# The order of the steps in the second block's layers: matrix-memory projections moved from the front to the last delta-rule chains

## The chip, the cores and the metric

One core of a Trainium2 chip runs the whole program. The metric is the device time of one execution in microseconds (us). The engines are TensorE (PE in the profile), VectorE (DVE), ScalarE (ACT), GpSimd (POOL) and SyncE (SP, which starts the DMAs). Each engine carries out its own instructions in a fixed order and waits, in that order, for what an instruction needs.

## The reference

The model has two parts. The first block (two layers of mixers and a mixture of 16 experts) is not touched by the change. The second block has two layers on a sequence of 256 tokens by 1024 features; each layer has two branches over the same input and then a feed-forward network, with layer norms. Branch A is a matrix memory (mLSTM, 4 heads, keys of 128, values of 256); branch B is a gated delta rule (8 heads of 128) on convolved projections. Cut to what matters:

```
def _mlstm_chunked(q, k, v, i_pre, f_pre):           # 4 heads, chunks of 64
    ... num = (q k^T * w) v + sc * (q C);  C = carry * C + k^T v ...
def _causal_conv(u, w):                              # 4 taps, per feature
    return lax.conv_general_dilated(u, ..., padding=[(k - 1, 0)], ...)
def _gated_delta_chunked(q, k, v, beta, g):          # 8 heads, chunks of 64
    q = _l2norm(q) * (dk ** -0.5)
    k = _l2norm(k)
    ...
    sol = lax.linalg.triangular_solve(eye + a_low, rhs, ...)   # per chunk of 64
    u, w = sol[..., :dv], sol[..., dv:]
    def step(s_st, chunk):                           # four chunks, one after another
        v_new = uc - w @ s_st
        o = qe @ s_st + attn @ v_new
        s_new = s_st * g_end + kd^T @ v_new
        return s_new, o
```

Everything is in float32.

## The kernel before

**Projections.** `gemm_t` (L72) makes one output tile of 256 features by 256 tokens with 48 matmuls: 8 pieces of the inner dimension, two halves, and three products each, because input and weight are each split into a high and a low part (`xh`, `xl`, and `whl`, which ACT and DVE make from the loaded weight at L62 and L63). The result is built in a PSUM tile `acc`; there are two such tiles in all, so that a third projection tile can begin only when the first has been read out by its evacuation.

**Steps.** A layer of `block2` first makes the gate rows (`small_rows`, a chain of short row operations), then goes through the steps of `ORDER2` (L1033), then `branches` (gates and products of both branches), `down`, `norm`, `ffn`, `norm`. The steps are:
- `G n` (`gdn_proj`): three projection tiles q, k, v of two delta-rule heads. `conv_piece` (L1146) evacuates each: two ACT and six DVE operations with the taps into the tile `cva`, a tanh on ACT, two DVE operations into `KQ`, `kr` or `vr`. `cva` has two buffers; for q and k POOL puts the squares in it (L1207), and step R reads them there.
- `Z n` (`gdn_gate`): one more projection tile, the output gate.
- `R n` (`gdn`): the delta-rule chain of that pair of heads. PE sums the squares (`pss`, L1232), then come products (`pk`, `py`, ...), then five levels of a triangular inverse (tile `pi`: L1310, a copy on ACT, L1315 and L1319, a subtraction on DVE), then `pu` (L1327) and `pw` (L1335), then four chunks of the recurrence (L1347, a subtraction on DVE, L1351, L1358, L1364, an update of the state on DVE), a norm on DVE and the transposes `pot` (L1380). Nearly every step waits for the one ahead of it on another engine.
- `P j` (`ml_proj`): the matrix memory's projections for two of its heads: tiles `qT` and `kT` (one buffer each, so the second pair's evacuations at L1396 and L1397 wait until the first pair's heads have been read), two tiles `va0` and `va1` of 512 features, and two gate tiles.
- `M j` (`mlstm`): the matrix memory of these two heads, one head after the other (`pb`, `pst`, `pkt`, `pd`, `pn`, squares into `junk` on ACT at L1471, a norm, `pha`).

`junk` is one tile that takes the squares of R (L1368) and of M (L1471), so that these writes follow in program order.

**What sets the order.** The program's text order gives priorities and the order of waits on shared buffers; a scheduler then writes one fixed list of instructions for each engine, in which the matmuls of a chain stand between those of projections. The object `after` holds back the first projection of the second layer until an operation of the norm ahead of it has been issued.

Of the kernel before, what the change touches and what calls it, by code (L numbers as in the profile page):

```python
# [1029 lines left out]
ALPHA = 4.0 ** 0.25  # L1030
D_FF = 2816
LN_EPS = 1e-5
ORDER2 = "P0 G0 G1 Z0 R0 Z1 R1 G2 Z2 G3 Z3 M0 R2 R3 P1 M1"  # L1033

QA, KA, VA, OA, QB, KB, VB, ZB, GA, GB = 0, 512, 1024, 2048, 3080, 4104, 5128, 6152, 7192, 8216

# [636 lines left out]
def split_x(E, x):  # L1673

    nc, m, C = E.nc, E.m, E.c2
    xh = E.st.tile([128, 8, 256], FR, name="xh", tag="st")
    xl = E.st.tile([128, 8, 256], FR, name="xl", tag="st")
    for k2 in range(4):
        pt = m.tile([128, 2, 256], FT, name="pln", tag="mm")
        for j in range(2):  # L1680
            for t in range(2):
                k = 2 * k2 + j
                nc.tensor.transpose(pt[:, j, 128 * t:128 * t + 128], x[:, t, 128 * k:128 * k + 128], C.id)
        ks = slice(2 * k2, 2 * k2 + 2)
        nc.scalar.activation(xh[:, ks], pt, AF.Copy)
        nc.vector.tensor_sub(xl[:, ks], pt, xh[:, ks])
    return xh, xl


def block2(E, x):  # L1690
    tc = E.tc
    xh, xl = split_x(E, x)
    nl = E.nlayers
    after = contextlib.nullcontext()
    for l in range(nl):
        with tc.tile_pool(name=f"t2_{l}", bufs=2) as E.t2, tc.tile_pool(name=f"sm{l}", bufs=2) as E.sm, \
                tc.tile_pool(name=f"rw{l}", bufs=1) as E.rows:
            E.P = E.rows
            G = G2(E, l, x, xh, xl)
            G.params()  # L1700
            G.junk = E.rows.tile([128, 256], FT, name="junk")
            G.R = small_rows(E, l, xh, xl)
            G.hbh = E.st.tile([128, 8, 256], FR, name="hbh", tag="st")
            G.hbl = E.st.tile([128, 8, 256], FR, name="hbl", tag="st")
            G.hah = E.st.tile([128, 8, 256], FR, name="hah", tag="st")
            G.hal = E.st.tile([128, 8, 256], FR, name="hal", tag="st")
            zs = {}
            for step in ORDER2.split():
                k, n = step[0], int(step[1])
                if k == "G":  # L1710
                    zs[n] = G.gdn_proj(n)
                elif k == "Z":
                    G.gdn_gate(n, zs[n])
                elif k == "R":
                    G.gdn(n, zs[n])
                elif k == "P":
                    with after:
                        zs["m", n] = G.ml_proj(n)
                    after = contextlib.nullcontext()
                else:  # L1720
                    G.mlstm(n, zs["m", n])
            G.branches()
        with tc.tile_pool(name=f"ffn{l}", bufs=1) as E.F, tc.tile_pool(name=f"lnp{l}", bufs=1) as E.lnp:
            ps = G.down(E.i["w_out_2"][l], G.yh, G.yl, KC)
            xh, xl = G.norm(0, ps)
            ps = G.ffn(xh, xl)
            r = G.norm(1, ps, l == nl - 1)
        if r:
            xh, xl = r
            after = G.after[0]  # L1730
# [70 lines left out]
def program(tc, ins, out):  # L1801
    nc = tc.nc
    E = Env()
    E.tc, E.nc, E.i, E.nlayers, E.nomoe = tc, nc, ins, 2, False
    with tc.tile_pool(name="c", bufs=1) as E.cp, tc.tile_pool(name="w", bufs=3) as E.wp, \
            tc.tile_pool(name="hl", bufs=3) as E.hl:
        xt = E.cp.tile([128, 2, D], FT, name="x")
        with tc.tile_pool(name="c1", bufs=1) as c1, tc.tile_pool(name="st1", bufs=4) as E.st, tc.tile_pool(name="md", bufs=1) as E.md, \
                tc.tile_pool(name="sm1", bufs=1) as E.sm:
            ct = c1.tile([128, 2, D], FT, name="xc")  # L1810

            def load_ctx():
                nc.sync.dma_start(ct, ins["ctx"].rearrange("(t p) d -> p t d", p=128))
                load_consts1(E, c1)

            E.load_x = lambda: nc.sync.dma_start(xt, ins["x"].rearrange("(t p) d -> p t d", p=128))
            E.load_ctx = load_ctx
            block1(E, [xt, ct])
        with tc.tile_pool(name="c2", bufs=1) as c2, tc.tile_pool(name="st2", bufs=6) as E.st, tc.tile_pool(name="pacc2", bufs=2, space=PSUM) as E.acc, \
                tc.tile_pool(name="pm2", bufs=2, space=PSUM) as E.m:  # L1820
            load_consts2(E, c2)
            E.out = out
            block2(E, xt)
# [16 lines left out]
```

## Time and profile before

| | |
|---|---|
| device time, median of 3 runs | 2824.7 us (2815.96 to 2825.24) |
| profiled execution: its own time | 2826.67 us |
| profiled execution: span | 2824.9 us |
| granted TensorE clock, mean over the span | 0.96 of full |
| busy: PE / DVE / ACT / POOL | 89% / 48% / 29% / 9% of the span |
| steps and branches, layer 0 | 1525.40 to 1944.80 us |
| steps and branches, layer 1 | 2169.70 to 2599.40 us |

The span is what the trace covers; the profiled execution took 1.8 us more, and 2 us more than the median of the runs. The two stretches at the end of the table are the ones in which the change moves anything. In the trace a row of the timeline gives start, length, engine, line and tile, and in square brackets how long the engine stood idle ahead of it and for whom. Ends of matmuls are modelled, so distances from start to start are used for PE.

### The profile page before, as it was taken

Reading aid. Unit: us, or ns where it says so; the run is one execution under the profiler, and the core shown is the slowest. Engines: PE = TensorE matmul, PEld = TensorE weight load, DVE = VectorE, ACT = ScalarE, POOL = GpSimd, SP = SyncE. Lnnn points to the kernel's source line nnn. Section 1 sums busy time; section 2 is a strip of 40 time slices with the busy share of each in tenths; the row PEclk is TensorE's granted clock in tenths of the full one; section 3 lists DMA queues with packets and bytes.
Section 4 is the critical chain, followed back from the end, with each engine's and each line's share of the span. In section 5 each row is a group of like instructions: output and inputs, shape, how many; then the busy total and the mean of one; then the engine's idle time right before and its main releaser. Section 6 shows DMA issues by size and latency. Waiting matters only on the chain.

```text
span 2824.9 us, 42465 instructions
## 1 busy us (share of the span) xinstructions
PE 2527.0 (89%) x17771; PEld 1740.5 (62%) x17771; DVE 1354.1 (48%) x2663; ACT 818.2 (29%) x1339; POOL 243.5 (9%) x293
## 2 busy tenths in 40 slices
PE   6999989988889997666667999999999999999998
PEld 4776743322227662111114988888997888879996
DVE  4446533232236562001103768456656667556765
ACT  2334311000014430000002434334444433334442
POOL 1000110000000010000000122000202031100200
PEclk9999999999999999888899998999999998999999
DMA  7434469999995568999996421335654431325553
GB/s 292 180 120 147 164 272 421 422 421 421 421 381 181 185 242 360 422 421 421 421 421 264 155 91 53 113 111 175 209 181 138 152 118 46 105 90 194 179 192 121
DMA packets 237459, 665.60 MB, mean 236 GB/s; under 512 B 11572, under 2 KB 165860, under 8 KB 182356
## 3 DMA queue, kind: packets, MB, share of 16 engines
q1 hardware_dynamic: 235428, 657.81, 61.2%
q0 software_dynamic: 1696, 4.59, 0.5%
q8 instruction: 139, 2.28, 0.3%
q14 instruction: 52, 0.43, 0.0%
q10 hardware_dynamic: 144, 0.49, 0.0%
HBM read 661.78 MB, written 1.05 MB: 235 GB/s over the span
## 4 chain that ended last, share of the span: by engine, by line
PE 59%; DMA 24%; issue 9%; DVE 5%; POOL 2%; ACT 1%; SPq 0%; DVEq 0%; ACTq 0%; POOLq 0%
DMA w<-in_exp_w_up 8%; DMA w<-in_exp_w_down 8%; PE acc L84 6%; PE acc L86 6%; DMA w<-in_exp_w_gate 6%; PE acc L85 6%; PE pj L316 3%; PE pj L318 3%; PE pgate L862 3%; PE pj L317 3%; PE pd L862 2%; PE pup L862 2%; PE pada L182 2%; PE psc L435 1%; PE psc L451 1%
## 5 line engine op out<-in xcount | busy, mean ns | idle before, releaser
L63 DVE TENSOR_TENSOR whl<-w,whl 128x1024 fp32r<-128x1024 f32 x376 | 469.2, 1251 | 310.0 <-ACT whl L62 309.4
L62 ACT ACTIVATE whl<-w 128x1024 fp32r<-128x1024 f32 x376 | 396.2, 1058 | 472.3 <-PE acc L86 237.0
L84 PE MATMUL acc<-xh,whl 128*128 128x256 f32 x1664 | 476.5, 286 | 0.5 <-DVE xh L1619 0.5
L86 PE MATMUL acc<-xh,whl 128*128 128x256 f32 x1664 | 471.7, 283 | 0.2
L85 PE MATMUL acc<-xl,whl 128*128 128x256 f32 x1664 | 471.1, 283 | 0.0
L84 PEld LDWEIGHTS acc<-xh,whl 128*128 128x128 f32 x1664 | 316.7, 190 | 11.0 <-issue 6.5
L86 PEld LDWEIGHTS acc<-xh,whl 128*128 128x128 f32 x1664 | 316.4, 190 | 5.6 <-issue 3.6
L85 PEld LDWEIGHTS acc<-xl,whl 128*128 128x128 f32 x1664 | 316.8, 190 | 3.3 <-issue 2.5
L862 PE MATMUL pup<-w,xg 128*64 128x512 f32 (+1 forms) x1024 | 221.4, 662 | 67.9 <-DMA w<-in_exp_w_up 67.9
L862 PE MATMUL pgate<-w,xg 128*64 128x512 f32 (+1 forms) x1016 | 218.5, 648 | 45.8 <-DMA w<-in_exp_w_gate 43.4
L862 PE MATMUL pd<-w,ehT 128*64 128x512 f32 (+1 forms) x1024 | 202.7, 622 | 59.3 <-DMA w<-in_exp_w_down 42.3
L862 PEld LDWEIGHTS pup<-w,xg 128*64 128x64 f32 (+1 forms) x1024 | 52.6, 130 | 228.7 <-DMA w<-in_exp_w_up 149.6
L862 PEld LDWEIGHTS pd<-w,ehT 128*64 128x64 f32 (+1 forms) x1024 | 51.7, 125 | 186.5 <-DMA w<-in_exp_w_down 87.2
L862 PEld LDWEIGHTS pgate<-w,xg 128*64 128x64 f32 (+1 forms) x1016 | 50.9, 127 | 177.7 <-DMA w<-in_exp_w_gate 91.8
L316 PE MATMUL pj<-whl,hT 128*128 128x256 f32 x496 | 144.5, 292 | 6.1 <-ACT hT L300 5.8
L318 PE MATMUL pj<-whl,hT 128*128 128x256 f32 x496 | 143.3, 290 | 0.9 <-DVE hT L301 0.9
L317 PE MATMUL pj<-whl,hT 128*128 128x256 f32 x496 | 142.8, 289 | 0.0
L893 DVE TENSOR_TENSOR od<-pd,g 128x512 f32<-128x512 f32 x24 | 16.6, 691 | 232.0 <-PE pd L862 232.0
L881 DVE SCALAR_TENSOR_TENSOR et<-et,pup 128x512 f32<-128x512 f32 x24 | 16.5, 687 | 224.0 <-PE pup L862 223.8
L316 PEld LDWEIGHTS pj<-whl,hT 128*128 128x128 f32 x496 | 94.5, 191 | 24.7 <-issue 10.9
L317 PEld LDWEIGHTS pj<-whl,hT 128*128 128x128 f32 x496 | 94.5, 191 | 13.1 <-issue 8.9
L318 PEld LDWEIGHTS pj<-whl,hT 128*128 128x128 f32 x496 | 94.5, 191 | 8.5 <-issue 5.7
(607 smaller groups left out, 4158.9 us busy)
## 6 DMA issues: line engine op xcount, KB each, us to landing
w<-in_exp_w_down SPq DMA_DIRECT2D x128, 1024.0 KB, 19.8
w<-in_exp_w_up SPq DMA_DIRECT2D x127, 1024.0 KB, 19.8
w<-in_exp_w_gate SPq DMA_DIRECT2D x125, 1024.0 KB, 19.8
w<-in_w_in SPq DMA_DIRECT2D x82, 1024.0 KB, 5.1
w<-in_ada_w SPq DMA_DIRECT2D x48, 1024.0 KB, 6.4
w<-in_w_ffn_up SPq DMA_DIRECT2D x44, 1024.0 KB, 5.1
w<-in_w_ffn_down SPq DMA_DIRECT2D x22, 1024.0 KB, 4.8
w<-in_w_out SPq DMA_DIRECT2D x16, 1024.0 KB, 5.5
```

The lines of the kernel that those rows point to most:

```text
L62: nc.scalar.activation(h, w, AF.Copy)
L63: (engine or nc.vector).tensor_sub(lo, w, h)
L84: nc.tensor.matmul(ps[:, b], h[:, k], xh[:, k], start=(k == 0), stop=False)
L85: nc.tensor.matmul(ps[:, b], h[:, k], xl[:, k], start=False, stop=False)
L86: nc.tensor.matmul(ps[:, b], lo[:, k], xh[:, k], start=False, stop=(k == KC - 1))
L182: nc.tensor.matmul(self.ps[32 * j:32 * j + 32], self.st[:, k], ws[j], start=(k == 0), stop=(k == KC - 1), skip_group_check=True)
L316: nc.tensor.matmul(ps, xh, wh, start=start, stop=False, skip_group_check=bool(ks))
L317: nc.tensor.matmul(ps, xh, wl, start=False, stop=False, skip_group_check=bool(ks))
L318: nc.tensor.matmul(ps, xl, wh, start=False, stop=stop, skip_group_check=bool(ks))
L435: self.E.nc.tensor.matmul(o, wT[:, 128 * c:128 * c + 128], v[:, t0 + c, 64 * h:64 * h + 64], start=(c == 0), stop=(c == n // 128 - 1))
L451: nc.tensor.matmul(ps[:, :n], self.cqT[r, h // 2, 128 * t:128 * t + 128], self.ckT[r, h // 2, k0:k0 + n], start=True, stop=True)
L862: m = nc.tensor.matmul(ps[64 * h + mw * i:64 * h + mw * i + mw], lhs(kk, i, e), ws[i][k][:, 512 * h:512 * h + 512], start=(kk == 0), stop= ...
```

## The change

In both layers P0 moves from the front to a place between R2 and R3, M0 moves behind R3, and R2 comes ahead of it; the steps G0 to Z3 stay in their own order. The hold-back `after` moves with the first projection, which is now G0's. (The changed file has one more line, so its lines from 1034 to 1709 are one higher.)

```diff
-ORDER2 = "P0 G0 G1 Z0 R0 Z1 R1 G2 Z2 G3 Z3 M0 R2 R3 P1 M1"
+
+ORDER2 = "G0 G1 Z0 R0 Z1 R1 G2 Z2 G3 Z3 R2 P0 R3 M0 P1 M1"
...
                 if k == "G":
-                    zs[n] = G.gdn_proj(n)
+                    with after:
+                        zs[n] = G.gdn_proj(n)
+                    after = contextlib.nullcontext()
...
                 elif k == "P":
-                    with after:
-                        zs["m", n] = G.ml_proj(n)
-                    after = contextlib.nullcontext()
+                    zs["m", n] = G.ml_proj(n)
```

No instruction of a step is added or removed. What moves on the engines is shown at three places, all in layer 0.

**Place 1, PE, the last part of R3.** Before, the values' projection of P1 (`va0_12669`) stands between the inverse levels of R2 and R3 (`pi_12046` and `pi_12301`):

```order
L94 MATMUL va0_12669<-whl_12673,xl_9410 128x512
L92 MATMUL va0_12669<-whl_12690,xh_9409 128x512
L93 MATMUL va0_12669<-whl_12690,xh_9409 128x512
L1310 MATMUL pi_12301<-XY_12285,Am_12299 64x64 x2
L1310 MATMUL pi_12046<-XY_11940,Am_12044 64x64 x8
L1310 MATMUL pi_12301<-XY_12285,Am_12299 64x64 x6
L92 MATMUL va1_12670<-whl_12673,xh_9409 128x512
L93 MATMUL va1_12670<-whl_12673,xh_9409 128x512
L94 MATMUL va1_12670<-whl_12673,xl_9410 128x512
```

In the changed program the same `va0_12669` stands behind the whole of R3: these rows are R3's last two chunks, its `pot`, the end of M0's first head (`pha`) and the start of its second (`pb`, `pst`, `pkt`), and then the first row of `va0`:

```order
L1365 MATMUL pO_12344<-vn_12347,at__12133 64x128 x2
L1359 MATMUL pS_12355<-vn_12347,kd_12096 128x128
L1348 MATMUL pO_12362<-S_12351,kb_12094 64x128 x2
L1352 MATMUL pO_12362<-S_12351,qe_12112 64x128 x2
L1365 MATMUL pO_12362<-vn_12365,at__12133 64x128 x2
L1381 MATMUL pot_12391<-cst0_98,vb_12092 128x128 x4
L1489 MATMUL pha_12466<-cst0_98,nm_12430 128x128
L1429 MATMUL pb_12474<-row_MS_9545,cst0_98 128x512
L1489 MATMUL pha_12466<-cst0_98,nm_12430 128x128 x3
L1442 MATMUL pst_12484<-qT_11740,kT_11741 128x128 x2
L1447 MATMUL pkt_12488<-cst0_98,kT_11741 128x128 x2
L92 MATMUL va0_12669<-whl_12673,xh_9409 128x512
```

The last projection matmul ahead of these (of P1's k tile, `acc_12613`) stands 40 rows earlier, ahead of R3's inverse from its second level on: 80 of R3's 112 `pi` matmuls, `pu`, `pw` and all four chunks lie between, with no projection among them (88 of 112 in layer 1).

**Place 2, ACT, the same part.** Before, the evacuation of P1's q tile (`qT_12549`) stands behind the first pair's last squares (L1471) among work of R3's levels (`T1`, L1312) and weight splits (L62):

```order
L62 ACTIVATE whl_12641<-w_12611 128x1024
L1471 ACTIVATE junk_9461,ssq_11816<-nm_11815 128x256
L1470 ACTIVATE nm_11815<-pn_11822 128x258
L1471 ACTIVATE junk_9461,ssq_11816<-nm_11815 128x256
L1312 ACTIVATE T1_11995<-pi_11986 128x256
L1279 ACTIVATE D1_12266<-D1_12266 128x256
L1281 ACTIVATE H_12264<-H_12264 128x256
L1396 ACTIVATE qT_12549<-acc_12555 128x512
L62 ACTIVATE whl_12673<-w_12671 128x1024
L1312 ACTIVATE T1_12025<-pi_12016 128x256
```

In the changed program the squares of R3's chunks (L1369, `ss_12313`) come first, then those of M0's first head (L1472), and behind them `qT_12549`:

```order
L1369 ACTIVATE junk_9461,ss_12313<-pO_12326 128x128
L1368 ACTIVATE vb_12092<-pO_12344 128x128
L1369 ACTIVATE junk_9461,ss_12313<-pO_12344 128x128
L1368 ACTIVATE vb_12092<-pO_12362 128x128
L1369 ACTIVATE junk_9461,ss_12313<-pO_12362 128x128
L1472 ACTIVATE junk_9461,ssq_12431<-nm_12430 128x256 x2
L1385 ACTIVATE hbh_9601<-gs_11335,gg_9457 128x512
L1434 ACTIVATE wt_12476<-wt_12476 128x256
L1493 ACTIVATE hah_9603<-gsA_11932 128x512
L1397 ACTIVATE qT_12549<-acc_12555 128x512
```

All write the one `junk_9461`. Until `qT_12549` and its like on DVE for `kT` have been carried out, P1's q and k tiles hold both `acc` tiles.

**Place 3, DVE, the start of the layer.** Before, the gate rows (`rows2`, `row_w1`, `row_g`) stand between weight splits (L63) and one evacuation of P0's (`kT_9606`):

```order
L1082 TENSOR_SCALAR row_w1_9531<-rows2_9519 40x256
L1086 SCALAR_TENSOR_TENSOR rows2_9519<-row_w1_9531,rows2_9519 40x256
L63 TENSOR_TENSOR whl_9746<-w_9744,whl_9746 128x1024
L1087 RECIPROCAL row_w1_9531<-row_w1_9531 40x256
L1397 COPY kT_9606<-acc_9669 128x512
L63 TENSOR_TENSOR whl_9763<-w_9761,whl_9763 128x1024
L1088 TENSOR_TENSOR rows2_9519<-rows2_9519,row_w1_9531 40x256
L1089 TENSOR_TENSOR rows2_9519<-rows2_9519 40x256
L1090 SCALAR_TENSOR_TENSOR rows2_9519<-rows2_9518,rows2_9519 40x256
L1091 TENSOR_SCALAR rows2_9519<-rows2_9519,ns_9529 40x256
L1093 SCALAR_TENSOR_TENSOR row_g_9540<-cst2_9407,rows2_9519 40x256
```

In the changed program the taps of G0's convolutions (L1157 on `cva_9665` and `cva_9736`) and their last step (L1161) stand between the same row operations:

```order
L1157 SCALAR_TENSOR_TENSOR cva_9736<-acc_9681,cw_9453,cva_9736 128x255
L63 TENSOR_TENSOR whl_9826<-w_9823,whl_9826 128x1024
L1089 TENSOR_TENSOR rows2_9519<-rows2_9519,row_w1_9531 40x256
L1157 SCALAR_TENSOR_TENSOR cva_9665<-acc_9610,cw_9453,cva_9665 128x253
L1157 SCALAR_TENSOR_TENSOR cva_9736<-acc_9681,cw_9453,cva_9736 128x254
L1090 TENSOR_TENSOR rows2_9519<-rows2_9519 40x256
L1157 SCALAR_TENSOR_TENSOR cva_9736<-acc_9681,cw_9453,cva_9736 128x253
L1161 SCALAR_TENSOR_TENSOR KQ_9605<-cvt_9674,cva_9665 128x4x64
L1091 SCALAR_TENSOR_TENSOR rows2_9519<-rows2_9518,rows2_9519 40x256
L1161 SCALAR_TENSOR_TENSOR KQ_9605<-cvt_9674,cva_9665 128x4x64
L1157 SCALAR_TENSOR_TENSOR cva_9736<-acc_9681,cw_9453,cva_9736 128x255
L1092 TENSOR_SCALAR rows2_9519<-rows2_9519,ns_9529 40x256
```

On PE, `pss` of R0 (which frees the first `cva`) stands behind G0's three tiles and G1's q tile, ahead of G1's k tile; before, P0's six tiles were ahead of G0.

## Rows read from the trace of the kernel before

**Rows 1.** Windows, steps and branches of both layers (window, length, busy by engine, PEclk, DMA).

```profile
1525.40:1944.80 419.40, 410.79 (x3791) 360.74 (x3792) 263.61 (x559) 171.02 (x296) 57.89 (x62) 0.96 0.35 112
2169.70:2599.40 429.70, 415.45 (x3785) 365.05 (x3786) 270.17 (x565) 171.99 (x297) 76.64 (x80) 0.95 0.34 111
```

**Rows 2.** Windows: bare tail of R0 and R1, layer 1 (busy: PE PEld DVE ACT POOL).

```profile
2332.80:2357.10 24.30, 22.76 (x214) 17.00 (x213) 12.19 (x41) 8.30 (x28) 0.00 (x0) 0.77 0.01 2
```

**Rows 3.** Timeline of PE, layer 1, inside the same tail (start, length, engine, line).

```profile
2333.48 0.68 PE L1310 MATMUL pi<-XY,Am 64*64 64x64 f32 x16
2334.09 0.44 PE L1351 MATMUL pO<-S,qe 128*64 128x128 f32 x4
...
2335.24 0.68 PE L1315 MATMUL pi<-T,XY 64*64 64x64 f32 x16
2335.76 0.63 PE L1319 MATMUL pi<-XY,T 64*64 64x64 f32 x16
...
2336.32 0.48 PE L1358 MATMUL pS<-vn,kd 64*128 64x128 f32 x2
...
2337.33 0.68 PE L1310 MATMUL pi<-XY,Am 64*64 64x64 f32 x16 [0.16 <-DVE XY L1320]
...
2341.14 1.09 PE L1327 MATMUL pu<-vb,XY 64*64 64x128 f32 x16
...
2347.05 0.69 PE L1347 MATMUL pO<-S,kb 128*64 128x128 f32 x4
...
2350.81 0.47 PE L1347 MATMUL pO<-S,kb 128*64 128x128 f32 x1
```

**Rows 4.** Timeline of PE, layer 1: the same level step at another clock.

```profile
2395.94 1.12 PE L1310 MATMUL pi<-XY,Am 64*64 64x64 f32 x16
2396.99 0.69 PE L1446 MATMUL pkt<-cst,kT 128*128 128x128 f32 x2
```

**Rows 5.** Timeline, layer 1: R3's last chunk and what follows.

```profile
2514.24 0.43 PE L1347 MATMUL pO<-S,kb 128*64 128x128 f32 x2
...
2520.35 1.12 PE L1380 MATMUL pot<-cst,vb 128*128 128x128 f32 x4 [4.49 <-DVE vb L1377]
...
2521.91 0.47 PE L1488 MATMUL pha<-cst,nm 128*128 128x128 f32 x1 [0.44 <-POOL nm L1484]
...
2522.31 2.07 PE L1428 MATMUL pb<-row_MS,cst 40*128 40x512 f32 x2
```

**Rows 6.** Windows: the projection right behind that, and one in the feed-forward network.

```profile
2525.40:2529.60 4.20, 4.20 (x22) 4.20 (x20) 2.64 (x4) 1.66 (x3) 0.00 (x0) 0.50 0.00 0
2645.00:2745.00 100.00, 100.00 (x860) 100.00 (x859) 61.99 (x63) 46.69 (x54) 7.08 (x8) 1.00 0.60 200
```

**Rows 7.** Windows, layer 0: beside the gate rows, then beside G0 to G2.

```profile
1538.00:1562.60 24.60, 24.60 (x202) 21.82 (x202) 20.19 (x33) 16.17 (x22) 0.30 (x1) 1.00 0.66 214
1568.00:1626.00 58.00, 57.89 (x470) 53.36 (x469) 47.90 (x95) 27.95 (x41) 12.46 (x12) 1.00 0.45 146
```

**Rows 8.** Windows, the first of these stretches: DVE's weight splits alone (line 63).

```profile
1538.00:1562.60 24.60, 10.83 (x9) 1.00 0.66 214
```

**Rows 9.** Tile cva: durations (ns, min/median/max) of its convolution operations, both layers.

```profile
L1156 DVE SCALAR_TENSOR_TENSOR cva<-acc,cw,cva x144: 462/477/486, 1580.0 to 2400.7; 128x255 f32<-128x255 f32 x48, 128x254 f32<-128x254 f32 x48, 128x253 f32<-128x253 f32 x48
...
L1160 DVE SCALAR_TENSOR_TENSOR KQ<-cvt,cva x16: 409/415/1265, 1588.8 to 2376.9; 128x256 f32<-128x256 f32 x16
```

**Rows 10.** Waits of engines, 2160 to 2215 us (total, times, longest).

```profile
PE va L92 <- ACT qT L1396: 3.8, 1, 3.8
ACT qT L1396 <- POOL x L1629: 3.4, 1, 3.4
```

**Rows 11.** Timeline of POOL at the start of layer 1.

```profile
2179.68 10.68 POOL L1629 TENSOR_TENSOR x<-x,gb 128x256 f32<-128x256 f32 x8
```

**Rows 12.** Timeline of PE: between chain and projection, layer 1.

```profile
2328.96 0.38 PE L85 MATMUL acc<-xl,whl 128*128 128x256 f32 x1
...
2330.33 0.38 PE L1315 MATMUL pi<-T,XY 64*64 64x64 f32 x5
```

**Rows 13.** Windows, layer 0: a stretch in mid-stage with waits.

```profile
1741.20:1749.00 7.80, 6.60 (x61) 5.79 (x59) 7.62 (x27) 3.19 (x7) 1.74 (x2) 0.78 0.01 2
```

## The prediction

> **What bounds the kernel now.** I read the windows over the two stretches of steps first, then the timeline of PE inside them, then the waits. In the windows [rows 1] PE is busy for 410.8 of 419.4 us and for 415.5 of 429.7 us, while DVE is busy for about 264 and 270, ACT for 171, POOL for 58 and 77 and the DMA share is 0.35. So PE sets the pace almost everywhere, and it stands idle for 8.6 + 14.2 = 22.8 us in both layers together. That is the ceiling on what a better order can win from idle time; beyond it there are only clock and switching. The reader should also see where the idle time sits. A chain by itself does not fill PE: in the bare tail of R0 and R1 [rows 2] 24.3 us pass with only 214 matmuls, and the granted clock is 0.77. Beside projections the same chains cost PE only their own matmuls. In the feed-forward network, where there are no chains, a projection matmul takes 100 / 860 = 0.116 us [rows 6]. So the question is not which work is done but what stands beside the delta-rule chains: a chain with projections beside it is cheap, one without is paid at its latency.
>
> **The change part by part.** Nothing is added or removed. Five terms follow from the order.
>
> *R3 becomes bare.* In the changed order of PE no projection stands between R3's second level and the end of M0's first head, since P1's q and k tiles hold both `acc` tiles. Their evacuations wait for M0's second head (one `qT`, one `kT`), this waits for M0's first, whose squares wait for `junk` behind R3's last. M0 and P1 thus queue up behind R3, not beside it. The length of this tail comes from the start-to-start distances in [rows 3] and [rows 5]: the rest of a level 2337.33 − 2335.24 = 2.09; two levels at 2337.33 − 2333.48 = 3.85, 7.70; the last level, 2341.14 − 2337.33 = 3.81; from `pu` to the first L1347 2347.05 − 2341.14 = 5.91; two chunks at 2350.81 − 2347.05 = 3.76, 7.52; from the last chunk's L1347 to `pha` 2521.91 − 2514.24 = 7.67; then `pb`, the product with `qT` and a copy until `va0` may start, an estimate of 3.5 from `pb`'s 2.07 at the lower clock [rows 5]. The sum is 38.2 us in layer 0. In layer 1 one more level step, 2335.24 − 2333.48 = 1.76, lies in it: 40.0. The mean is 39.1.
>
> What these matmuls would cost beside projections is subtracted, since before they are paid so. A level's three pieces take 0.61 + 0.52 + 0.56 = 1.69 us for 48 records [rows 3]; the order counts half as many, as the trace shows two records for each of these. The 80 `pi` matmuls of the tail are therefore 80 / 24 × 1.69 = 5.6 us, and the other 64 (128 records at about 0.11, from L1351's 0.44 for four) 14. That is 19.6, and the excess is 39.1 − 19.6 = 19.5 per layer. Lower bound: in the bare tail of R0 and R1 [rows 2] half the 214 records are `pi` (about 112, 3.9 us) and the others 11.2, so its excess is 24.3 − 15.1 = 9. There a second chain fills in; R3 has only the last of R2 beside it, so I stay near 19.5. Upper bound: at half clock a level step takes 2396.99 − 2395.94 = 1.05 us instead of 0.61 [rows 4]; over the tail's levels that adds some 4, to 24. I take 20. After the tail the projections resume at a lower clock: behind the bubble in today's order 22 matmuls took 4.20 us at 0.50 [rows 6], where 22 × 0.116 = 2.6 would do, so +2 (1.6 and some for the rise). 22 per layer, **+44**.
>
> The Trainium skill, "TensorE: Matmul & The Clock Gate", Part 1, says that the array's default is the throttled state, 1.2 GHz, and that only activity releases 2.4 GHz. The 0.50 behind the bubble agrees. Taken strictly the rule puts the whole tail at the lower level, where I put only its second half; the sum would then be that of the half-clock rival below.
>
> *Today's bubble goes.* Before, R3's end has a bubble of its own: from 2514.24 to 2529.60 [rows 5, 6], 15.4 us, with some 6 us of matmuls in it (`pot`, `pha`, `pb` and 22 projections). After, M1 stands there beside the gates of branch B. −9 per layer, **−18**. If M1 were not covered there, up to 9 would come back.
>
> *Start of layer 0.* The gate rows' chain now shares DVE with G0's convolutions. Window 1538 to 1562.6 [rows 7]: DVE busy 20.19 in 24.6 us, of which 10.83 are nine splits [rows 8], some 0.6 is P0's evacuation, so the rows need 8.7. A convolution needs 6 × 0.477 + 2 × 0.415 = 3.7 us of DVE [rows 9]. Until G1's k tile may begin, DVE must do three convolutions (11.1), the rows (8.7), ten or eleven splits (12.5) and about 1.5 of small work behind `pss`, 34 us. PE has in this time four tiles, 4 × 48 × 0.116 = 22.3, and some 4.7 of `pss`, `pk`, `pb` and row transposes: 27. So it waits 7, and 3 more go to the lower clock on resumption and to `cva`: with two buffers G0's third convolution waits for `pss`, which stands behind G1's q tile. **+10**. Bounds: 0, if DVE does the rows late as it does everything else, and 13, if the third convolution begins only at `pss`. Nearest to 0 is window 1568 to 1626 [rows 7], where DVE is busy 47.9 of 58 beside convolutions and PE loses nothing; it has no rows in it, so I stay by the sum.
>
> *Start of layer 1.* The first new tile waits for POOL's update of x, which ends at 2179.68 + 10.68 = 2190.4 [rows 11]. Today this hits `qT`, and PE waits 3.8 us for it behind ACT's 3.4 [rows 10]. After, it hits the first `cva`, behind which 10 us of DVE work for convolution, rows and splits still stand before the next `acc` is free, where `qT` needed one 0.6 us copy: 9 us later than now, then the second wait as in layer 0 (some 6), less part of the present 3.8, plus 2 of clock. **+13**; bounds 0 and 17. With some rise of the clock after each stall (2 per layer) the two starts together are **+27**.
>
> *Fewer switches and waits in mid-stage.* By the order, the number of passages from a chain piece back to projections falls from 87 to 71 in layer 0 and from 86 to 74 in layer 1. At such a place ten projection matmuls took 2330.33 − 2328.96 = 1.37 us instead of 1.16 [rows 12], 0.2 each: **−5.6**. Mid-stage stretches with a lower clock, such as 1741.2 to 1749.0 at 0.78 [rows 13], lie where the steps are now otherwise mixed; I take 2 per layer off, **−4**.
>
> The sum is 44 − 18 + 27 − 5.6 − 4 = +43. The profiled execution, 2826.67, is 2 us above the median, so the forecast is 2824.7 + 43, rounded **2868 us**.
>
> **The rivals.** *The tail is cheap.* Its excess is that of R0's and R1's tail, 9 and 1 for the clock, not 22: for it speaks that R2's last chunks fill in at first; against it that R3's own levels wait on ACT, DVE and POOL just as [rows 3] shows. 2868 − 2 × 12 = 2844.
>
> *The starts cost nothing.* DVE has 5 to 10 us of slack in every stretch [rows 7] and splits run ahead. Against it stands the serial wait on `cva` and POOL's end in layer 1. 2868 − 27 = 2841.
>
> *Half clock throughout.* The tail with so little in it drops to the lower level from its first waits on, and the resumption is slow: +5 for the levels, +2 more behind, in each layer, and starts at their bounds (+3): 2868 + 14 + 3 = 2885, up to 2895 if the projections behind the starts also crawl.
>
> *The other side: mixing costs more than I count.* If each passage between chain and projection cost not 0.2 but (43 + 5.6) / 28 = 1.7 us, the 28 that go would pay for everything and the time would be that of before, 2825; from 2 us on it would be faster. [rows 12] speaks against it, and so does the idle total: all that PE loses in both layers is 22.8 us [rows 1]. For it speaks only that lower clocks [rows 13] don't count as idle.
>
> **How the numbers follow.** About 0.5% (14 us) is what a measurement of this kernel can tell from no change. Chances: the forecast, 2850 to 2884, 0.62; the cheap tail 0.11; the free starts 0.11; half clock 0.10; the other side 0.06. The bound for slower is 2838.8. The forecast and half clock lie above it wholly, the cheap tail and the free starts mostly (0.05 of their 0.22 below), so slower has 0.88, within 0.5% 0.08 and faster 0.04. The range 2838 to 2895 reaches over all cases but the other side and the ends of the next ones.
>
> **What would show it.** In the new trace of PE: R3's levels with idle time at each `pi` (released by DVE `XY` and ACT `T1`), no row of L84 or L92 between them for 36 to 42 us in each layer, granted clock 0.5 to 0.8 there, and `va0` right behind `pkt`. At the start of each layer a wait of PE for `acc` behind a `cva` operation, 5 to 10 us in layer 0 and more in layer 1. At the end no bubble of 15 us before the gates of branch B. The windows of both layers should last some 440 and 453 us. I am wrong if the tail is under 30 us, if PE never waits at the starts, or if M1's heads stand bare at the end, which would put the time above my range.

## The result and the profile after

The changed kernel takes 2859.7 us (median of 4 runs, 2858.6 to 2860.9) against 2824.9 us before: a ratio of 1.0132, 95% interval 1.0118 to 1.0146. It is slower by 35 us; forecast were 43 us more, 2868, with 2838 to 2895 as the range. The profiled execution took 2860.33 us, its span is 2858.5 us.

The windows of the changed kernel that answer to [rows 1], [rows 2], [rows 5] and [rows 7] (length, busy PE, PEld, DVE, ACT, POOL, then PEclk, DMA share, GB/s): both layers' steps; the start of layer 0; the bare tail of R0 and R1; the bare tail of R3 in layer 0, what follows it, and the tail in layer 1; and M1 at the end of layer 0. The two windows of R3's tail run from the first piece of its inverse behind the last projection to the first `va0`, as the forecast counted it.

```profile
1522.05:1963.32 441.27, 417.57 (x3791) 367.42 (x3791) 266.54 (x559) 171.26 (x296) 59.16 (x62) 0.91 0.32 105
2184.39:2628.80 444.41, 413.85 (x3790) 365.12 (x3791) 271.62 (x565) 173.91 (x300) 75.28 (x80) 0.92 0.32 105
1540.00:1582.00 42.00, 32.82 (x253) 31.01 (x252) 30.72 (x71) 16.32 (x26) 7.63 (x6) 0.76 0.30 97
1650.00:1680.00 30.00, 28.02 (x236) 20.77 (x236) 10.99 (x36) 9.24 (x32) 0.00 (x0) 0.67 0.05 18
1793.28:1832.02 38.74, 27.50 (x276) 17.90 (x275) 18.40 (x71) 9.57 (x31) 2.55 (x3) 0.72 0.12 41
1832.00:1837.30 5.30, 5.28 (x18) 4.08 (x18) 1.39 (x3) 0.00 (x0) 0.00 (x0) 0.80 0.01 3
2451.72:2497.37 45.65, 32.69 (x299) 22.15 (x295) 18.71 (x72) 10.31 (x35) 3.71 (x4) 0.62 0.08 25
1894.00:1920.00 26.00, 26.00 (x206) 23.62 (x205) 16.39 (x35) 10.11 (x14) 1.83 (x2) 1.00 0.41 133
```

The layers' matmuls, to within 5 as many as in [rows 1], take 441.3 and 444.4 us; some 440 and 453 were forecast. (These windows run from the first `pln` to the first matmul of `down`; between the same two instructions the layers of before take 419.4 and 429.5 us.) R3 stands bare for 38.7 and 45.7 us, at a clock of 0.72 and 0.62. The bubble of [rows 5] is gone: where M1 stands beside branch B's gates PE is busy throughout at full clock.

The timeline of PE shows the start and the end of the bare tail, layer 0 (start, length, engine, line, tile; in brackets the idle time ahead and for whom):

```profile
1792.30 0.28 PE L86 MATMUL acc<-xh,whl 128*128 128x256 f32 x1
...
1793.28 0.68 PE L1316 MATMUL pi<-T,XY 64*64 64x64 f32 x16
...
1795.67 0.68 PE L1311 MATMUL pi<-XY,Am 64*64 64x64 f32 x16 [0.88 <-DVE XY L1321]
...
1799.20 0.68 PE L1311 MATMUL pi<-XY,Am 64*64 64x64 f32 x16 [1.17 <-DVE rst_a L39]
...
1819.71 0.69 PE L1365 MATMUL pO<-vn,at__12133 64*64 64x128 f32 x4
1824.89 1.11 PE L1381 MATMUL pot<-cst,vb 128*128 128x128 f32 x4 [4.49 <-DVE vb L1378]
1826.46 0.47 PE L1489 MATMUL pha<-cst,nm 128*128 128x128 f32 x1 [0.46 <-POOL nm L1485]
1826.87 2.07 PE L1429 MATMUL pb<-row_MS,cst 40*128 40x512 f32 x2
...
1831.12 0.63 PE L1447 MATMUL pkt<-cst,kT 128*128 128x128 f32 x2
1832.02 0.79 PE L92 MATMUL va<-whl,xh 128*128 128x512 f32 x1 [0.26 <-ACT qT L1397]
```

The last projection matmul is at 1792.30, the next at 1832.02, and it waited for the evacuation of `qT`. The timeline of ACT says why that came so late:

```profile
1773.40 0.39 ACT L1471 ACTIVATE nm<-pn 128x258 f32<-128x258 f32 x1 [2.48 <-PE pn L1469]
...
1778.58 0.39 ACT L1471 ACTIVATE nm<-pn 128x258 f32<-128x258 f32 x1 [0.20 <-PE pn L1469]
...
1820.63 0.27 ACT L1369 ACTIVATE junk<-pO 128x128 f32<-128x128 f32 x1
1820.78 0.20 ACT L1369 ACTIVATION_READ_ACCUMULATOR junk<-pO 128x1 f32 x1
1821.02 0.42 ACT L1472 ACTIVATE junk<-nm 128x256 f32<-128x256 f32 x1
...
1831.37 0.60 ACT L1397 ACTIVATE qT<-acc 128x512 f32<-128x512 f32 x1
```

What M0's squares read, `nm`, is there from 1778.58 at the latest. The squares (L1472) begin more than 42 us later, at 1821.02, right behind R3's last (L1369), on the shared `junk`; the rest of M0's first head, `pb` and `qT` come behind them.

The waits of the changed kernel at the starts, for PE in layer 0 (1540 to 1582 us), and for layer 1, from the timeline, ACT's first convolution operation, the gate row that DVE finishes and PE's longest wait; they answer to [rows 10]:

```profile
PE acc L84 <- DVE cva L1157: 4.9, 1, 4.9
PE acc L84 <- DVE rst_a L40: 4.3, 1, 4.3
```

```profile
2207.70 0.84 ACT L1154 ACTIVATE cva<-acc,cw 128x256 f32<-128x256 f32 x2 [2.51 <-POOL x L1630]
...
2213.34 0.67 DVE L1094 TENSOR_TENSOR_SCAN row_g<-cst,rows 40x256 f32<-40x256 f32 x1
...
2214.11 1.12 PE L1133 MATMUL ps_tok<-cst,row_g 40*64 40x4 f32 x13 [8.92 <-issue]
```

In layer 0 PE waits twice for an `acc` tile behind DVE; in layer 1 the first convolution starts only when POOL's update of x is done, and PE's longest wait, 8.92 us, is ahead of the transposes `ps_tok` of the gate row `row_g`. The profile names no releaser for it; DVE ends `row_g` 0.1 us before, behind the first taps.

**Where the time went.** For each group of matmuls of one tile and shape I took the distance from its start to the next group's, less what such a group takes in the kernel before where nothing holds it up (its lower fifth there; 0.116 us for a projection matmul). From `pln` to `down` the matmuls' own time so found is 368.3 us in each layer of each kernel; what is above it is called loss here. Before, the layers lose 51.1 and 61.2 us, after 73.0 and 76.1, so +36.8. (The profiled execution's first block was 3.4 us shorter, and the feed-forward layers differ by 0.2; 36.8 − 3.4 + 0.2 = 33.6 is the difference of the spans.) By place:

| loss, us (layer 0, layer 1) | before | after | difference | forecast |
|---|---|---|---|---|
| start, to R0's first `pi` | 5.4, 16.8 | 19.9, 22.2 | +20 | +27 |
| R0's and R1's levels and tail | 10.9, 11.2 | 13.3, 8.8 | 0 | 0 |
| mid-stage beside projections | 23.2, 20.1 | 11.9, 11.6 | −20 | −9.6 |
| R3's bare tail | none | 21.1, 26.7 | +48 | +44 |
| the end (bubble, then B's gates) | 11.5, 13.1 | 6.6, 6.8 | −11 | −18 |

(Each kernel's losses come from its one profiled execution. The runs of one kernel spread over 2 to 17 us in its set, and kernel 1's and kernel 9's profiled executions were 5 us faster than their medians; so differences of a few us in a loss are not more than a hint. The expectations below were written with a rougher count, each group by its single matmuls, whose losses are larger by a constant; differences between kernels are the same in both.)

### The profile page after: what moved, and what is told of

Same layout as the page of the kernel before. It is cut to its first block, busy times and chain, and to the rows that moved or that the text cites. A ratio compares the mean times of both kernels' runs of the same rounds, so it can differ in the third digit from the quotient of the medians.

```text
span 2858.5 us, 42501 instructions
## 1 busy us (share of the span) xinstructions
PE 2532.3 (89%) x17771; PEld 1748.5 (61%) x17771; DVE 1360.3 (48%) x2663; ACT 819.3 (29%) x1339; POOL 244.0 (9%) x293
## 4 chain that ended last, share of the span: by engine, by line
PE 60%; DMA 24%; issue 8%; DVE 4%; ACT 2%; POOL 1%; SPq 0%; DVEq 0%; ACTq 0%; POOLq 0%
DMA w<-in_exp_w_up 9%; DMA w<-in_exp_w_down 8%; PE acc L84 7%; PE acc L86 7%; PE acc L85 7%; DMA w<-in_exp_w_gate 5%; PE pj L316 3%; PE pj L318 3%; PE pj L317 3%; PE pgate L862 3%; PE pd L862 3%; PE pup L862 2%; PE pada L182 2%; DMA w<-in_w_in 1%; PE psc L435 1%
## 5 line engine op out<-in xcount | busy, mean ns | idle before, releaser
L63 DVE TENSOR_TENSOR whl<-w,whl 128x1024 fp32r<-128x1024 f32 x376 | 470.5, 1253 | 322.7 <-ACT whl L62 322.4
L62 ACT ACTIVATE whl<-w 128x1024 fp32r<-128x1024 f32 x376 | 396.5, 1057 | 505.6 <-PE acc L86 259.8
L84 PEld LDWEIGHTS acc<-xh,whl 128*128 128x128 f32 x1664 | 320.3, 192 | 27.6 <-issue 22.8
L86 PEld LDWEIGHTS acc<-xh,whl 128*128 128x128 f32 x1664 | 319.7, 192 | 2.3 <-issue 1.1
L862 PE MATMUL pd<-w,ehT 128*64 128x512 f32 (+1 forms) x1024 | 211.5, 655 | 58.3 <-DMA w<-in_exp_w_down 41.2
L862 PE MATMUL pgate<-w,xg 128*64 128x512 f32 (+1 forms) x1016 | 212.0, 628 | 39.8 <-DMA w<-in_exp_w_gate 36.9
L893 DVE TENSOR_TENSOR od<-pd,g 128x512 f32<-128x512 f32 x24 | 16.6, 691 | 236.6 <-PE pd L862 236.6
L316 PEld LDWEIGHTS pj<-whl,hT 128*128 128x128 f32 x496 | 94.2, 190 | 24.4 <-issue 10.9
```

Source lines behind the costliest of these rows:

```text
L62: nc.scalar.activation(h, w, AF.Copy)
L63: (engine or nc.vector).tensor_sub(lo, w, h)
L84: nc.tensor.matmul(ps[:, b], h[:, k], xh[:, k], start=(k == 0), stop=False)
L86: nc.tensor.matmul(ps[:, b], lo[:, k], xh[:, k], start=False, stop=(k == KC - 1))
L316: nc.tensor.matmul(ps, xh, wh, start=start, stop=False, skip_group_check=bool(ks))
L862: m = nc.tensor.matmul(ps[64 * h + mw * i:64 * h + mw * i + mw], lhs(kk, i, e), ws[i][k][:, 512 * h:512 * h + 512], start=(kk == 0), stop= ...
```

## The experiments

All times are medians beside runs of the kernel before on the same chip (2823.2, 2825.7 and 2821.4 us in the three sets); losses are given as start and rest, layer 0 / layer 1.

| kernel | time, us | ratio to before (95%) | start | rest |
|---|---|---|---|---|
| before | 2824.9 | | 5.4 / 16.8 | 45.7 / 44.4 |
| changed | 2859.7 | 1.0132 (1.0118 to 1.0146) | 19.9 / 22.2 | 53.1 / 53.9 |
| 1 changed, scratch tiles apart | 2830.7 | 1.0026 (1.0014 to 1.0037) | 21.0 / 24.9 | 33.6 / 35.4 |
| 2 before, G0 ahead of P0 | 2833.7 | 1.0032 (1.0020 to 1.0043) | 17.1 / 16.0 | 44.8 / 43.4 |
| 3 changed, P0 in front | 2830.9 | 1.0028 (1.0015 to 1.0041) | 5.6 / 18.1 | 49.4 / 49.4 |
| 4 before, P0 behind R1 | 2837.6 | 1.0052 (1.0037 to 1.0067) | 19.9 / 25.1 | 41.4 / 41.6 |
| 5 before, scratch tiles apart | 2815.3 | 0.9971 (0.9958 to 0.9983) | 13.0 / 16.6 | 41.0 / 35.9 |
| 6 both, 1 and 3 | 2815.9 | 0.9970 (0.9952 to 0.9988) | 7.0 / 18.4 | 35.3 / 40.1 |
| 7 changed, `pss` early | 2868.2 | 1.0162 (1.0133 to 1.0191) | 17.3 / 21.7 | 58.7 / 58.0 |
| 8 changed, gate rows later | 2859.2 | 1.0128 (1.0100 to 1.0155) | 19.6 / 20.1 | 52.9 / 50.4 |
| 9 kernel 1, Z0 Z1 in front | 2819.0 | 0.9990 (0.9980 to 1.0000) | 14.7 / 14.3 | 38.6 / 36.9 |
| 10 kernel 6, M0 between R2 and R3 | 2814.4 | 0.9975 (0.9964 to 0.9986) | 13.0 / 18.2 | 35.1 / 43.1 |

**1. Is it the shared scratch tile that makes R3 bare?**

```diff
             G.junk = E.rows.tile([128, 256], FT, name="junk")
+            G.junk2 = E.rows.tile([128, 128], FT, name="junk2")
...
-            nc.scalar.activation(self.junk[:, 0:128], po[:, 0], AF.Square, accum_out=ss[:, c:c + 1])
+            nc.scalar.activation(self.junk2, po[:, 0], AF.Square, accum_out=ss[:, c:c + 1])
```

> The changed kernel, with a scratch tile of its own for R's squares (128 columns), so that M0's squares need not stand behind R3's. If this one shared tile is what holds M0 and so P1's values behind R3 (my reading), the bare run of R3 goes from PE's order and most of its excess with it: 29 and 35 us of PE's time over its matmuls were lost there, of which some 12 per layer would be lost beside projections too. Expected 2860 - 2 x 18 = about 2824, between 2815 and 2835. Rival: the chain's latency is paid whether projections stand beside it or not; then no more than 5 us per layer come back and the time stays above 2850.

Measured 2830.7, in the expected range. The rest loses 33.6 and 35.4 instead of 53.1 and 53.9 us, 19 less per layer (the profiled execution was 5 us faster than the median); the start is as dear as before the edit. A window of this kernel from inside R3, about as long as the tail of the changed kernel, and its timeline of PE:

```profile
1793.40:1831.60 38.20, 38.20 (x345) 30.87 (x344) 23.53 (x60) 15.94 (x28) 2.69 (x4) 1.00 0.40 129
```

```profile
1801.93 0.40 PE L94 MATMUL va<-whl,xl 128*128 128x512 f32 x1
1802.25 0.68 PE L1316 MATMUL pi<-T,XY 64*64 64x64 f32 x16
1802.77 0.63 PE L1320 MATMUL pi<-XY,T 64*64 64x64 f32 x16
1803.33 0.70 PE L1454 MATMUL pd<-vm,kw 64*128 64x258 f32 x2
...
1805.17 0.50 PE L92 MATMUL va<-whl,xh 128*128 128x512 f32 x1
```

And ACT, where M0's first squares stood 42 us behind their input:

```profile
1772.88 0.39 ACT L1471 ACTIVATE nm<-pn 128x258 f32<-128x258 f32 x1 [0.20 <-PE pn L1469]
1773.30 0.42 ACT L1472 ACTIVATE junk<-nm 128x256 f32<-128x256 f32 x1
```

PE is busy for all of the 38.2 us at full clock, with 345 matmuls where there were 276 in 38.7, and `va` stands beside `pi` and M0's `pd`. The squares follow their input at once. One scratch tile that nobody reads tied M0 and P1 to R3's end.

**2. Is the start a loss of its own?** Against the kernel before, with the hold-back on G0 as in the changed kernel:

```diff
-ORDER2 = "P0 G0 G1 Z0 R0 Z1 R1 G2 Z2 G3 Z3 M0 R2 R3 P1 M1"
+ORDER2 = "G0 P0 G1 Z0 R0 Z1 R1 G2 Z2 G3 Z3 M0 R2 R3 P1 M1"
```

> The old order with G0 alone ahead of P0 (G0 P0 G1 ..., the rest as before). If the start of a layer is a loss of its own (G0's convolutions beside the gate rows on DVE, cva with two buffers, POOL's update of x in layer 1), which the traces put at 15 and 6 us, the time rises by 15 to 20 to about 2842, with no change behind R1. Rival: the start only loses because P0 is not there to cover; with P0 right behind G0 the rise is under 6 us, 2825 to 2831.

Measured 2833.7: between the two, below what I expected and above the rival. The start of layer 0 loses 11.7 us more than before, layer 1 0.8 less, and the rest loses 1 less in each. So one delta projection in front is enough for most of layer 0's loss, with P0 right behind it. In layer 1 G0 alone loses nothing; both orders meet POOL's update of x there, but that this is the reason is not shown.

**3. P0 left at the front.** Against the changed kernel, with the hold-back on P0 as before:

```diff
-ORDER2 = "G0 G1 Z0 R0 Z1 R1 G2 Z2 G3 Z3 R2 P0 R3 M0 P1 M1"
+ORDER2 = "P0 G0 G1 Z0 R0 Z1 R1 G2 Z2 G3 Z3 R2 R3 M0 P1 M1"
```

> The new order with P0 left at the front (P0 G0 ... R2 R3 M0 P1 M1). The start should cost nothing against before (20 us less than the changed kernel), but R2 and R3 now run together without P0's projections: 245 and 237 chain matmuls in a row without a projection instead of 146 and 159. By the bare tail's rate of about 0.12 us lost for each, 10 us more per layer. Expected 2860 - 20 + 20 = about 2860, 2850 to 2868. Rival: the start is the larger part of the loss, and the tail's length hardly matters; then about 2840.

Measured 2830.9, below the range and below the rival's 2840. The start costs what it did before, as expected (5.6 and 18.1). But the rest did not get dearer by 10 per layer; it lost 4 less. The window of the bare run in layer 0:

```profile
1760.50:1811.20 50.70, 41.26 (x477) 29.01 (x476) 21.87 (x81) 14.38 (x46) 3.28 (x4) 0.77 0.09 29
```

It is longer, 50.7 us, and holds 477 matmuls; the loss in it is 20.6 us, no more than the 21.1 in the 38.7 us of the changed kernel. R2 and R3 run side by side here, and each fills some of the other's waits. My rate per matmul was wrong: a bare run loses latency, and two chains in step lose it once.

**4. P0 beside R0's and R1's tail.** Against the kernel before, again with the hold-back on G0:

```diff
-ORDER2 = "P0 G0 G1 Z0 R0 Z1 R1 G2 Z2 G3 Z3 M0 R2 R3 P1 M1"
+ORDER2 = "G0 G1 Z0 R0 Z1 R1 P0 G2 Z2 G3 Z3 M0 R2 R3 P1 M1"
```

> The old order with P0 behind R1 (G0 G1 Z0 R0 Z1 R1 P0 G2 ... M0 R2 R3 P1 M1): the start is that of the changed kernel (+20), and P0's projections stand where both kernels have R0's and R1's tail bare, which loses 19 and 15 us there. If projections beside a tail win back some 60% of what it loses (12 per layer), the time is 2825 + 20 - 24 = about 2821, 2812 to 2832. Rival: a tail costs the same beside projections; then 2845.

Measured 2837.6, outside the range and nearer the rival. The start costs what the changed kernel's does, in layer 1 some 3 us more; the rest loses only 3 to 4 us less per layer than before, where 12 were expected. R0's and R1's tail is no longer bare. What stays bare is R3's end, for 9.3 us in each layer (windows of both):

```profile
1873.20:1882.50 9.30, 4.37 (x17) 1.81 (x16) 5.25 (x31) 2.27 (x8) 1.82 (x2) 0.72 0.00 0
2528.90:2538.20 9.30, 4.36 (x17) 1.79 (x15) 5.25 (x31) 2.27 (x8) 1.82 (x2) 0.70 0.00 1
```

About 7 us are lost there, and still 41 in all: a chain beside projections goes on losing time, so covering a tail gives back only a part.

**5 and 6. Apart in the old order; both causes taken away.** The scratch tiles of kernel 1 in the kernel before, and in the order of kernel 3.

> The kernel before, with a scratch tile of its own for R's squares. If the shared tile ties M's squares to R's wherever they meet, also in the old order (M0's stand ahead of R2's, M1's first behind R3's last, in the bubble at the end), both come free: M0's second head can stand in the bare tail of R0 and R1, and the bubble of 8 to 10 us per layer at R3's end shrinks. Expected 2823 - 2 x 8 = about 2807, between 2800 and 2815. Rival: the tie only hurts where the order puts M0 behind R3; then 2820 to 2825.

> The new order with P0 left at the front and the scratch tiles apart: both causes of the loss taken away at once. By the parts of the traces (PE's time over its matmuls: start 9 and 21 us with P0 in front, the rest about 80 with the tiles apart) the two layers lose 190 us against 211 before: 2823 - 20 = about 2803, 2795 to 2815. Rival: with R2 and R3 running together (2831 with one tile, where I had expected 2860) there is nothing left for the tiles to give, and the time stays above 2823.

Both are faster than before by 0.3%. Kernel 5, 0.3 us outside its range: the tie was there in the old order too; the rest loses 4.7 and 8.5 us less, and the bare stretch at R3's end shrinks from 10.1 us to some 4 in each layer. But the start of layer 0 loses 7.6 more (its first `pi` comes 8 us later; kernel 10 loses the same 13.0 there; why is open). Kernel 6 is faster than the changed kernel by 44 us, but 1 us outside the range I gave: the rest loses 35.3 and 40.1, not as little as hoped in layer 1, where R3's end stays bare for 8.7 us:

```profile
2511.10:2519.80 8.70, 3.19 (x18) 1.79 (x17) 5.74 (x23) 1.88 (x5) 1.83 (x2) 0.71 0.00 0
```

With one cause taken away the other remains (2830.7 and 2830.9); with both away nothing of the loss is left. The two don't add: each alone gives back 29 us, both together 44.

**7 and 8. What makes the start dear?** Kernel 7 writes `pss` and its reader into `gdn_proj`, between the second projection and the third (v); kernel 8 calls `small_rows` between G0 and G1.

```diff
         gemm_t(E, [self.cols(QB + 256 * hp), self.cols(KB + 256 * hp)], self.xh, self.xl, ev)
+        p_ = "ab"[hp % 2]
+        pss = E.m.tile([128, 2, 4], FT, name="pss", tag="m" + p_)
...
+        z.nn = nn = E.sm.tile([128, 8], FT, name="nn", tag="nn" + p_)
+        nc.vector.tensor_scalar(nn, pss.rearrange("p a b -> p (a b)"), 1e-6, None, op0=OP.add)
         gemm_t(E, [self.cols(VB + 256 * hp)], self.xh, self.xl, lambda j, ps: conv_piece(E, cw, 16 + 2 * hp, ps, z.vr))
         return z
```

```diff
-            G.R = small_rows(E, l, xh, xl)
...
             for step in ORDER2.split():
                 k, n = step[0], int(step[1])
+                if G.R is None and (k, n) == ("G", 1):
+                    G.R = small_rows(E, l, xh, xl)
```

> The changed kernel, with the sums of squares (pss, and the one DVE operation that reads them) written into the projection step instead of the chain, so that the buffers of cva come free earlier. If it is the wait of G0's third convolution for a cva that stands behind G1's q tile which makes the start dear, 6 to 8 us per layer come back: about 2846, 2840 to 2850. Rival: it is DVE's share between gate rows and convolutions; then at most 2 per layer, above 2855.

> The changed kernel, with the gate rows written behind G0's projections instead of ahead of them, so that the convolutions go first on DVE. If the start is dear because the rows hold up the convolutions on DVE, 5 to 10 us per layer come back: about 2845, 2838 to 2852. Rival: the wait on cva decides; then the rows' order changes little, 2855 to 2865, and a later start of R0's products could even cost some us.

Neither gave back what was expected. Kernel 7 is slower by 8 us than the changed one, within its rival's bound: the start wins 2.6 and 0.5 us, and the chains behind it, whose order the scheduler made anew, lose 4 to 6 more. In layer 0 G0's third convolution does begin earlier, 37.6 us behind the first `pln` instead of 47.6, and yet hardly anything comes back (PE now waits 2.0 us at `pss`, for the squares on POOL). So the wait for `cva` is not what makes the start dear. Kernel 8 has the time of the changed one, which is the rival's; its reason, that the wait on `cva` decides, does not fit kernel 7. The waits of PE in its start (1536 to 1600 us):

```profile
PE ps_tok L1133 <- DVE rst_a L39: 7.4, 1, 7.4
...
PE ps_rows L1051 <- ACT whl L62: 1.6, 1, 1.6
```

The wait for `acc` is gone, and 7.4 us are spent instead on the gate rows' transposes: with the convolutions first the rows are late, with the rows first the convolutions are. Putting one ahead of the other only moves the wait.

**9. Something light in front.** Kernel 1 with another order, and `gdn_gate` able to run ahead of `gdn_proj` (both get an empty record made in advance; the hold-back is on Z0):

```diff
-ORDER2 = "G0 G1 Z0 R0 Z1 R1 G2 Z2 G3 Z3 R2 P0 R3 M0 P1 M1"
+ORDER2 = "Z0 Z1 G0 G1 R0 R1 G2 Z2 G3 Z3 R2 P0 R3 M0 P1 M1"
```

> The changed order with the scratch tiles apart (2831) and the two gate tiles Z0 and Z1 ahead of G0. If a layer's start is dear because the first projections have a long evacuation on DVE (a convolution each) while the gate rows need DVE too, 11 us of projections with one DVE operation each cover the rows: the start's loss, 25 and 28 us, falls by 10 or more in each layer. R0 and R1 then have less beside them (232 and 167 chain matmuls in a row instead of 115), which by the run with R2 and R3 together costs little, 5 us per layer. Expected 2831 - 20 + 10 = about 2821, 2812 to 2828. Rival: the loss belongs to the convolutions wherever they stand (DVE needs longer for such a tile than PE); then nothing is won and R0's and R1's longer bare run makes it 2832 to 2842.

Measured 2819.0, as expected. The starts lose 6 and 11 us less, where 10 or more were expected in each layer; the rest loses 5 and 1.5 more, in layer 0 this lies behind R0 and R1, not in them as expected. Two tiles with one DVE operation each in front give DVE the time for the rows. With kernel 8 this speaks for the sum of DVE's work, not for one wait in it; it is argued from the two runs, not shown.

**10. M0's place.** Kernel 6 with another order:

```diff
-ORDER2 = "P0 G0 G1 Z0 R0 Z1 R1 G2 Z2 G3 Z3 R2 R3 M0 P1 M1"
+ORDER2 = "P0 G0 G1 Z0 R0 Z1 R1 G2 Z2 G3 Z3 R2 M0 R3 P1 M1"
```

> P0 in front, scratch tiles apart, M0 written between R2 and R3. With the tiles apart the place of M0 in the text should matter little, since the scheduler lets it start as soon as its projections are there in both: 2816 as with M0 behind R3, 2810 to 2822. Rival: M0's rank ahead of R3 frees P1's buffers earlier and covers more of R3: below 2808.

Measured 2814.4, the same as kernels 5 and 6 within the intervals, as expected: once the tie is cut, M0's place in the text matters little. No kernel here beats 5, 6 and 10 by more than can be measured; 5 is the smallest edit of before that beats it.

## Why the prediction was right, point by point

**R3 becomes bare: right, and the reason was right.** The tail was predicted at 38.2 us in layer 0 and measured at 38.7 (window above); in layer 1 at 40.0, measured 45.7. There one `pi` waits 2.16 us for R2's norm on DVE, and the clock fell to its lower level earlier (last section); what each of the two costs was not parted:

```profile
2459.67 0.68 PE L1311 MATMUL pi<-XY,Am 64*64 64x64 f32 x16 [2.16 <-DVE rsy_a L41]
```

The excess was set at 20 and 2 per layer; the loss is 21.1 and 26.7, and about 1 us in the 18 matmuls behind it (clock 0.80 in the 5.3 us window). Kernel 1 shows that the tie through `junk` makes it.

**The Trainium skill's rule.** "TensorE: Matmul & The Clock Gate", Part 1, has the throttled state as the default, which taken strictly would have put the whole tail at 1.2 GHz and the sum at 2885. The granted clock in the tail was 0.72 in layer 0 and 0.62 in layer 1, so the first part of it still ran at the higher level (`pi` x16 in 0.68 us at 1799.20, as in [rows 3]). The measurement decides for something in between: in layer 0 nearly what the forecast assumed, the second half at the lower level, in layer 1 more than that.

**The start: right in kind, mis-sized and partly misplaced.** Forecast 10 and 13, with 4 for the clock; measured 14.5 and 5.4. In layer 0 the sum of DVE's work against PE's (34 against 27 us) is what kernels 8 and 9 speak for. The further step, that the third convolution waits for `pss` through `cva`, is there, but kernel 7 gives back only 2.6 us with it; that fits the bound of 13 set for it, 3 above the forecast, and not the 6 to 8 expected of kernel 7. In layer 1 PE's long wait is, other than forecast, not for `acc` but for the gate row. I charged the whole new wait there and took off too little of what was there already: before, that start loses 16.8 us, three times layer 0's, and kernel 2 shows that G0 in front adds nothing to it.

**The mid-stage: a sentence that does not hold, and a move that was not counted.** "Beside projections the same chains cost PE only their own matmuls" does not hold. Before, the chains lose 23.2 and 20.1 us in the long stretch beside projections, and kernel 4, where only 9.3 us per layer stay bare, still loses 41 behind the start. By my count of the gaps by the tiles at either end, a passage into a chain piece and back costs some 0.3 us there, and the rest lies within the chains. But this is not why the credit was 20 us where I had 9.6. R3 has left the stretch, and heads of the matrix memory have moved too: before, two of the four stood in it (M0's second and M1's first), after, one (M0's first). Gaps at one of their tiles make 6 us of the loss there in each layer before and 0.7 after. About 11 of the 20 us are theirs, and most of that comes back in the last row of the table, where three heads stand now instead of one. Without them the mid-stage gives some 9, as forecast.

**The bubble at the end: right.** The bubble itself, with 10.4 us lost in each layer, is gone (clock 1.00 in the last window): −21, where I had −18. What is left of the row, some +9 for both layers, is what the two heads more lose behind the tail; of that I had counted only the 2 per layer at the resumption.

**How much of it was luck.** Measured less forecast, start, mid-stage, tail and end were off by −7, −10, +4 and +7 us, together −6; against the medians the forecast was 8 us too high. The −10 and the +7 are for the most part the one move of these heads, seen at two places. The rest, +4 at the tail against −7 at the starts, cancels by luck, as layer 0's start (2.5 above its 12) does in part against layer 1's (10 below its 15). The other-side rival, that a passage between chain and projection costs several times 0.2 us, would need 1.7 us each where the traces show some 0.3.

## What to carry to other kernels

A write-only scratch tile that two chains share is an edge between them like any other: look for it before moving a chain, for it can queue up one behind the whole of the other, and through the buffers behind it also the work that was meant as cover. Count what is lost in a stretch by latency and not by matmuls, and count it also where projections stand beside the chain. Count every chain that moves both where it leaves and where it comes to. At the start of a layer, put ahead what is light on the engine that the preparations need.

## What the runs showed of the hardware

In a bare tail the granted clock did not fall to its lower level at once. Windows of the changed kernel, R3's tail in layer 0 and in layer 1, each in two parts:

```profile
1793.28:1810.20 16.92, 12.36 (x219) 9.86 (x218) 8.73 (x26) 4.50 (x14) 0.72 (x1) 1.00 0.29 94
1810.30:1832.02 21.72, 15.14 (x57) 8.04 (x57) 9.58 (x45) 4.99 (x17) 1.83 (x2) 0.50 0.00 0
2451.72:2462.20 10.48, 6.93 (x148) 5.60 (x146) 6.34 (x22) 2.32 (x10) 1.89 (x2) 1.00 0.33 103
2462.30:2497.37 35.07, 25.66 (x155) 16.46 (x151) 12.27 (x51) 7.99 (x25) 1.82 (x2) 0.50 0.00 1
```

In layer 0 it stayed at 1.00, the higher level, for 16.9 us, in layer 1 for 10.5, and was at 0.50, the lower one, from there to the end of the tail, with 57 matmuls in 21.7 us and 155 in 35.1. With two chains side by side (kernel 3, 477 matmuls in 50.7 us) the mean was 0.77, against 0.72 and 0.62 here. So a second chain fills waits; that it also holds the clock up is only argued from these three numbers.
